# Smaller pieces for the preparation of lambda's powers, B's coefficients and the gate's scan in the first projection

## The chip, the cores and the metric

The kernel runs on one core of a Trainium2 chip. The metric is the device time of one execution in microseconds (us). The core has one in-order queue for each engine: PE (TensorE, the matmuls), DVE (VectorE), ACT (ScalarE), POOL (GpSimd) and SP (SyncE, which issues most DMAs). An engine starts the next instruction of its queue when that one's inputs are there; whatever stands behind a waiting instruction waits too.

## The reference, cut to what matters

Two layers over a sequence of 256 frames with a model width of 2048: first a gated linear attention (GLA), then a diagonal state-space layer (S5). Each layer modulates its input by a conditioning vector (adaLN), widens it to 4096, and ends in a residual LayerNorm.

```python
mod = einsum('bd,lde->lbe', silu(c), ada_w) + ada_b
for i in range(2):
    shift, scale, gate = split(mod[i], 3)
    u = x * (1 + scale) + shift
    h = gla_mixer(u, ...) if i == 0 else s5_mixer(u, ...)
    x = layer_norm(alpha * x + (1 + gate) * h, ln_g[i], ln_b[i])

# gla_mixer: the first projection, and the gate
q, k, v, z, g_lr = split(u @ w_in, ...)          # w_in: 2048 x 10256
log_alpha = log_sigmoid(g_lr @ gate_w2 + gate_b) / 16
# per chunk of 64 frames: cum = cumsum(log_alpha), k_dec = k * exp(tot - cum), ...

# s5_mixer: what can be prepared from the weights alone
dt = exp(log_dt)
mag = exp(a_re * dt)
lb_re, lb_im = mag * cos(a_im * dt), mag * sin(a_im * dt)      # lambda
coef = ((lb - 1) * conj(a)) / |a|^2                             # coef_re, coef_im
bb = coef * (b_re + 1j * b_im)                                  # B's coefficients
```

Everything is in float32 and has to be that exact, so each product is made from parts of reduced width (below).

## The kernel before, in words

The weights of every projection come in tiles of 128 x 1024 (two blocks of 128 input channels, k-blocks, by 512 output columns, 512 KB) through a ring of four buffers. Each tile is split into a high part `hi`, a copy made by ACT (L145), and a low part `lo = w - hi`, a subtraction on DVE (L146). PE then makes three products from them: `uh*hi`, `uh*lo`, `ul*hi`, where `uh` and `ul` are the same two parts of the modulated input. `hi` and `lo` have three buffers each. A tile of v is 12 matmuls of 512 columns (`mv_step`, L167 hi, L168 lo, L169 `ul`), a tile of q, k or z 24 matmuls of 256 columns (`st_step`, L180, L181, L182, of which L182 reads `lo`).

The first projection takes 96 tiles, called 0 to 95 here, in four blocks of u's 16 k-blocks (2, 2, 4 and 8 k-blocks), since u becomes available in this order. The third block is tiles 24 to 47: v in 24 to 39, q and k in 40 to 47. The fourth is tiles 48 to 95: q and k in 48 to 63, v in 64 to 95. At the end of each column group PE's sums are added to SBUF by DVE: `vbig` (L403) for v, `qk` (L417) for q and k. After tile 95 the attention scores (`psst`) and the z tiles follow.

Around the tiles the kernel hands over other work in pieces, in the Python loop that issues the tiles:

```python
            with tc.issue_after(last_lo[0]), tc.issue_after(last_mm[0]):
                for g_ in along.get(j, ()):
```

- `along`: the adaLN product (`psa`, `modsum`, `mods`) and the transposes of u (`psx`, `uf`, `u0l`), at fixed tiles.
- `lam`, a generator (`prep_lambda`): one piece after each tile of the third block. It works out lambda, its powers 1 to 8 (`pwr`, by the helper `tt`, L513, with scratch `pwt`), the coefficients (`crci`) and the packed eighth power (`psl`). `expx` is its exponential.
- `bg`, a list of pieces popped at a rate (`pump(V_RATE)`, in the fourth block): B's coefficients (`prep_b`, tiles `bb` and `bt`), their transposes (`psrb`), those of C, lambda's powers in rows (`prep_pow`, `pd`, `pspw`, `lc`), and weight sums of the later adaLN.
- `gate`, a generator (`gla_gate`): one piece a tile from the twentieth tile of the fourth block. Its scans along time are L739.

A piece ends at a `yield` (or at the end of a list's function). What is inside one piece is issued in one go; a scheduler then orders each engine's queue by when the inputs are expected to be ready, with the order of issue as its rule between ready ones. So the pieces decide which DVE instructions stand ahead of the `lo` of which tile.

Of the kernel before, what the change touches and what calls it, by code (L numbers as in the profile page):

```python
# [11 lines left out]
ALU = mybir.AluOpType  # L12
# [21 lines left out]
def trunk(ctx, tc, x, c, ln_g, ln_b, ada_w, ada_b, gla_w_in, gla_gate_w2, gla_gate_b, gla_norm_g,  # L34
# [3 lines left out]
    V, S, PE = nc.vector, nc.scalar, nc.tensor  # L38
# [35 lines left out]
    def s8t(name, shape, dt=F32):  # L74
        return s8.tile([P] + shape, dt, tag="s8", name=name)
# [382 lines left out]
    got = []  # L458
# [25 lines left out]

    SM = {}

    def expx(o, a, t1, t2, ti):

        V.tensor_scalar(a, a, 88.0, -87.0, op0=ALU.min, op1=ALU.max)
        V.tensor_scalar(t1, a, 1.4426950408889634, MAGIC, op0=ALU.mult, op1=ALU.add)  # L490
        V.tensor_scalar(t1, t1, MAGIC, None, op0=ALU.subtract)
        V.scalar_tensor_tensor(t2, t1, -0.693359375, a, op0=ALU.mult, op1=ALU.add)
        V.scalar_tensor_tensor(t2, t1, 2.12194440e-4, t2, op0=ALU.mult, op1=ALU.add)
        V.tensor_scalar(ti, t1, 127.0, 8388608.0, op0=ALU.add, op1=ALU.mult)
        V.tensor_scalar(o, t2, 1.9875691500e-4, 1.3981999507e-3, op0=ALU.mult, op1=ALU.add)
        for cf in (8.3334519073e-3, 4.1665795894e-2, 1.6666665459e-1, 5.0000001201e-1, 1.0, 1.0):
            V.tensor_tensor(o, o, t2, op=ALU.mult)
            V.tensor_scalar(o, o, cf, None, op0=ALU.add)
            if cf == 5.0000001201e-1:
                yield  # L500
        V.tensor_tensor(o, o, ti.bitcast(F32), op=ALU.mult)

    def prep_lambda():
        st = s8t("lamst", [16, 128])
        pw = s8t("pwr", [8, 2, 128])
        n_ = [0]

        def new():
            n_[0] += 1
            return st[:, n_[0] - 1, :]  # L510

        def tt(o, a, b, op):
            V.tensor_tensor(o, a, b, op=op)  # L513

        ar, ai = new(), new()
        dma(ar.rearrange("g (t p) -> g t p", t=2), s5_a_re[0].rearrange("(t g) p -> g t p", g=P))
        dma(ai.rearrange("g (t p) -> g t p", t=2), s5_a_im[0].rearrange("(t g) p -> g t p", g=P))
        dtt = tp.tile([P, 2], F32, tag="dtt", name="dtt", bufs=1)
        ld = tp.tile([2, P], F32, tag="ld", name="ld", bufs=1)
        dma(ld, s5_log_dt[0].rearrange("(t g) -> t g", g=P))  # L520
        for _ in range(3):
            yield
        ps = psx("psld")
        PE.transpose(ps[:, 0:2], ld, ident[:2, :2])
        sm = tp.tile([P, 4, 2], F32, tag="sm", name="sm", bufs=1)
        smi = tp.tile([P, 130], mybir.dt.int32, tag="smi", name="smi", bufs=1)
        S.copy(sm[:, 0], ps[:, 0:2])
        yield from expx(dtt, sm[:, 0], sm[:, 1], sm[:, 2], smi[:, 128:130])
        yield
        ag, mg, th = new(), new(), new()  # L530
        for t in range(2):
            V.tensor_scalar(ag[:, t * 64:t * 64 + 64], ar[:, t * 64:t * 64 + 64], dtt[:, t:t + 1], None, op0=ALU.mult)
            V.tensor_scalar(th[:, t * 64:t * 64 + 64], ai[:, t * 64:t * 64 + 64], dtt[:, t:t + 1], None, op0=ALU.mult)
        nn, r = new(), new()
        yield from expx(mg, ag, nn, r, smi[:, 0:128])
        yield
        V.tensor_scalar(nn, th, 1.0 / TWO_PI, MAGIC, op0=ALU.mult, op1=ALU.add)
        V.tensor_scalar(nn, nn, MAGIC, None, op0=ALU.subtract)
        V.scalar_tensor_tensor(r, nn, -C1, th, op0=ALU.mult, op1=ALU.add)
        V.scalar_tensor_tensor(r, nn, -C2, r, op0=ALU.mult, op1=ALU.add)  # L540
        V.scalar_tensor_tensor(r, nn, -C3, r, op0=ALU.mult, op1=ALU.add)
        V.tensor_scalar(r, r, 3.1415925, -3.1415925, op0=ALU.min, op1=ALU.max)
        sn, sh = new(), new()
        S.activation(sn, r, AF.Sin)
        S.activation(sh, r, AF.Sin, scale=0.5)
        yield
        cosm = new()
        tt(cosm, sh, sh, ALU.mult)
        V.tensor_scalar(cosm, cosm, -2.0, 1.0, op0=ALU.mult, op1=ALU.add)
        lr, li = pw[:, 0, 0, :], pw[:, 0, 1, :]  # L550
        tt(lr, mg, cosm, ALU.mult)
        tt(li, mg, sn, ALU.mult)
        nr, den, t1, t2 = new(), new(), new(), new()
        crci = tp.tile([P, 2, 128], F32, tag="crci", name="crci", bufs=1)
        cr, ci = crci[:, 0], crci[:, 1]
        V.tensor_scalar(nr, lr, -1.0, None, op0=ALU.add)
        tt(den, ar, ar, ALU.mult)
        tt(t1, ai, ai, ALU.mult)
        tt(den, den, t1, ALU.add)
        V.reciprocal(den, den)  # L560
        yield
        tt(t1, nr, ar, ALU.mult)
        tt(t2, li, ai, ALU.mult)
        tt(cr, t1, t2, ALU.add)
        tt(cr, cr, den, ALU.mult)
        tt(t1, li, ar, ALU.mult)
        tt(t2, nr, ai, ALU.mult)
        tt(ci, t1, t2, ALU.subtract)
        tt(ci, ci, den, ALU.mult)

        tm = s8t("pwt", [2, 4, 128])
        for m in (1, 2, 4):
            a_r, a_i = pw[:, 0:m, 0, :], pw[:, 0:m, 1, :]
            b_r = pw[:, m - 1:m, 0, :].to_broadcast([P, m, 128])
            b_i = pw[:, m - 1:m, 1, :].to_broadcast([P, m, 128])
            o_r, o_i = pw[:, m:2 * m, 0, :], pw[:, m:2 * m, 1, :]
            x1, x2 = tm[:, 0, 0:m, :], tm[:, 1, 0:m, :]
            tt(x1, a_r, b_r, ALU.mult)
            tt(x2, a_i, b_i, ALU.mult)
            tt(o_r, x1, x2, ALU.subtract)  # L580
            tt(x1, a_r, b_i, ALU.mult)
            tt(x2, a_i, b_r, ALU.mult)
            tt(o_i, x1, x2, ALU.add)
            yield
        SM.update(pw=pw, cr=cr, ci=ci)

        ps = psx("psl8")
        idv = ident.rearrange("g (f q b) -> g f q b", q=4, b=2)
        pv = ps[:, 0:256].rearrange("p (r h t n) -> p r h t n", r=2, h=2, t=2)
        for ri in range(2):  # L590
            for h in range(2):
                for t in range(2):
                    for q in range(4):
                        PE.matmul(pv[32 * q:32 * q + 32, ri, h, t, :],
                                  lhsT=pw[:, 7, ri, t * 64 + h * 32:t * 64 + h * 32 + 32], rhs=idv[:, :, q, :],
                                  start=True, stop=True)
        pr = ps[:, 0:256].rearrange("p (r k t n) -> p r t k n", r=2, k=2, t=2)
        for j, r, s in ((0, 0, 1.0), (0, 1, 1.0), (1, 0, 1.0), (1, 1, -1.0)):
            S.mul(l8[:, :, j, r].rearrange("p t (k n) -> p t k n", k=2), pr[:, j], s)
# [35 lines left out]
    def prep_b(t):  # L635
        got = {}

        def load():
            bi = s8t(f"bin{t}", [2, 64, 16])
            got["bi"] = bi  # L640
            dma(bi[:, 0], s5_b_re[0, t * P:(t + 1) * P])
            dma(bi[:, 1], s5_b_im[0, t * P:(t + 1) * P])

        def comp():
            bi = got["bi"]
            bb = s8t(f"bb{t}", [2, 64, 16])
            tm = s8t(f"bt{t}", [64, 16])
            cr = SM["cr"][:, t * 64:t * 64 + 64].unsqueeze(2).to_broadcast([P, 64, 16])
            ci = SM["ci"][:, t * 64:t * 64 + 64].unsqueeze(2).to_broadcast([P, 64, 16])
            V.tensor_tensor(bb[:, 0], bi[:, 0], cr, op=ALU.mult)  # L650
            V.tensor_tensor(tm, bi[:, 1], ci, op=ALU.mult)
            V.tensor_tensor(bb[:, 0], bb[:, 0], tm, op=ALU.subtract)
            V.tensor_tensor(bb[:, 1], bi[:, 1], cr, op=ALU.mult)
            V.tensor_tensor(tm, bi[:, 0], ci, op=ALU.mult)
            V.tensor_tensor(bb[:, 1], bb[:, 1], tm, op=ALU.add)
            got["b"] = bb.rearrange("g r p i -> g (r p) i")

        return [load], [comp] + to_rows(lambda: got["b"], lambda s, i: s[:, :, i], t, 256, f"b{t}")

    def prep_c(t):  # L660
        got = {}
# [23 lines left out]
    for part in range(2):  # L685
        for j in range(4):
            bg.extend(ada_dve(1, part, j))
    V_RATE, Z_RATE, OP_RATE = 0.62, 0.944, 0.755
    KEEP = (4, 6)
    GATE_AT = 20  # L690
    SCAN_RATE = 1.728
# [4 lines left out]
    def gla_gate():  # L696
# [20 lines left out]
        for f2 in range(4):  # L717
            ps = psx(f"psla{f2}")
            for i in range(2):
                f = 2 * f2 + i  # L720
                PE.matmul(ps[:, i * T:(i + 1) * T], lhsT=w2[:, f * P:(f + 1) * P], rhs=glr, start=True, stop=True)
            for i in range(2):
                f = 2 * f2 + i
# [13 lines left out]
        V.memset(rmask.rearrange("p (c t) -> p c t", c=4)[:, :, 0:1], 0.0)  # L737
        for f in range(8):
            V.tensor_tensor_scan(ea[:, f, :], rmask, la[:, f, :], 0.0, op0=ALU.mult, op1=ALU.add)  # L739
            if f == 3:  # L740
                yield
        yield
        cum = ea.rearrange("p f (c t) -> p (f c) t", c=4)
# [89 lines left out]
    for c0, w_, o in ((0, 4, 0), (1, 3, 4), (2, 2, 7)):  # L833
        a = s8t(f"qs{c0}", [8, w_, 64])
# [78 lines left out]
    for g in range(8):  # L913
# [9 lines left out]
        for f in range(4):  # L923
            i = (g * 4 + f) % 8
# [531 lines left out]
```

## Time and profile before

| what | value |
|---|---|
| time, median of 3 runs | 1836.67 us (1836.52 to 1839.31) |
| profiled execution | 1838.83 us, span 1837.1 us, mean granted clock 0.991 |
| PE busy | 1781.8 us (97%) |
| DVE busy | 1410.3 us (77%) |
| ACT busy | 895.4 us (49%) |
| POOL busy | 88.0 us (5%) |
| DMA | mean 249 GB/s, 457.86 MB |

The span is the time from the first to the last instruction, and the time of the execution is a little longer. Busy times are sums over instructions; a row of a timeline gives the start, the duration, the engine, the source line, the operation with what it writes and reads, and in brackets the idle time of the engine before it with what ended it. Rows of the timeline that stand next to each other overlap somewhat, because the engines are pipelined: the step from one start to the next says what an instruction costs in a row of them.

### The profile page before, as it was taken

How to read it: one execution, taken by the hardware profiler on the slowest of the kernel's cores; microseconds unless marked ns; L12 is line 12 of the kernel's file. 1: busy time of each engine (PE TensorE's matmuls, PEld its weight loads, DVE VectorE, ACT ScalarE, POOL GpSimd, SP SyncE). 2: the span in 40 equal slices, each digit the busy share in tenths (PEclk: the TensorE clock that was granted, in tenths of full speed). 3: DMA queues.
4: the chain of work that ended last, by engine and by line, in shares of the span. 5: the costliest groups of instructions: out<-in, count | busy, mean ns of one | idle time of the engine just before them, and what ended most of it. 6: DMA issues, size and time to landing. Idle time of an engine off the chain costs nothing.

```text
span 1837.1 us, 33664 instructions
## 1 busy us (share of the span) xinstructions
PE 1781.8 (97%) x13491; PEld 1574.5 (86%) x13491; DVE 1410.3 (77%) x1880; ACT 895.4 (49%) x1266; POOL 88.0 (5%) x94
## 2 busy tenths in 40 slices
PE   7999999999999999999999999999999999999997
PEld 5776897899999888899998999988888888888886
DVE  4887757879999988687699689888577775557556
ACT  4433557556556333654554535545445444444332
POOL 0000000000000000002233300000000000000000
PEclk9999999999999999999999999999999999999998
DMA  9997975879889998486665577999688886668653
GB/s 343 387 342 247 294 247 162 284 258 325 290 289 321 335 356 289 160 264 204 194 202 168 170 213 217 234 246 233 218 278 269 275 271 208 187 192 324 194 185 92
DMA packets 246101, 457.86 MB, mean 249 GB/s; under 512 B 19828, under 2 KB 49198, under 8 KB 244662
## 3 DMA queue, kind: packets, MB, share of 16 engines
q1 hardware_dynamic: 239320, 436.02, 74.1%
q0 software_dynamic: 5856, 18.63, 3.1%
q8 instruction: 106, 1.74, 0.4%
q10 hardware_dynamic: 768, 1.05, 0.2%
q14 instruction: 51, 0.42, 0.1%
HBM read 437.01 MB, written 18.61 MB: 248 GB/s over the span
## 4 chain that ended last, share of the span: by engine, by line
PE 78%; DVE 11%; DMA 4%; issue 3%; ACT 2%; POOL 0%; SPq 0%; DVEq 0%; ACTq 0%; POOLq 0%
PE gl L192 13%; PE gl L193 7%; PE op L168 6%; PE op L169 6%; PE op L167 6%; PE z L182 3%; PE z L181 3%; PE z L180 3%; PE v L168 3%; PE v L169 2%; PE v L167 2%; PE su L180 2%; PE su L181 2%; PE su L182 2%; PE sz L180 2%
## 5 line engine op out<-in xcount | busy, mean ns | idle before, releaser
L146 DVE TENSOR_TENSOR logl<-wgl,higl 128x1024 fp32r<-128x1024 f32 x128 | 156.7, 1224 | 116.0 <-ACT higl L145 111.2
L145 ACT CAST higl<-wgl 128x1024 fp32r<-128x1024 f32 x128 | 134.4, 1051 | 172.4 <-PE gl L192 167.5
L192 PE MATMUL gl<-yp,higl 128*128 128x512 f32 x512 | 179.4, 395 | 0.1
L192 PE MATMUL gl<-yb,higl 128*128 128x512 f32 x512 | 179.1, 395 | 0.0
L145 ACT CAST hio<-wo 128x1024 fp32r<-128x1024 f32 x95 | 100.2, 1055 | 152.8 <-PE op L169 131.9
L146 DVE TENSOR_TENSOR loo<-wo,hio 128x1024 fp32r<-128x1024 f32 x95 | 116.5, 1228 | 66.8 <-ACT hio L145 64.8
L317 DVE SCALAR_TENSOR_TENSOR acc<-wa,cs,acc 128x512 f32<-128x512 f32 x217 | 162.7, 750 | 2.9 <-DMA wa<-in_ada_w 0.2
L180 PE MATMUL sz<-u1h,hisz 128*128 128x256 f32 x512 | 150.4, 294 | 2.3 <-ACT zs L1284 2.3
L180 PE MATMUL su<-u1h,hisu 128*128 128x256 f32 x512 | 151.3, 297 | 0.0
L180 PE MATMUL z<-u0h,hiz 128*128 128x256 f32 x512 | 148.7, 290 | 0.0
L182 PE MATMUL sz<-u1h,losz 128*128 128x256 f32 x512 | 144.5, 283 | 2.1 <-DVE losz L146 2.1
L182 PE MATMUL su<-u1h,losu 128*128 128x256 f32 x512 | 145.8, 285 | 0.0
L181 PE MATMUL su<-u1l,hisu 128*128 128x256 f32 x512 | 145.6, 284 | 0.0
L182 PE MATMUL z<-u0h,loz 128*128 128x256 f32 x512 | 144.9, 283 | 0.6 <-DVE loz L146 0.6
L181 PE MATMUL z<-u0l,hiz 128*128 128x256 f32 x512 | 144.7, 283 | 0.0
L181 PE MATMUL sz<-u1l,hisz 128*128 128x256 f32 x512 | 144.7, 283 | 0.0
L193 PE MATMUL gl<-yb,logl 128*128 128x256 f32 x512 | 143.0, 279 | 0.0
L193 PE MATMUL gl<-yp,logl 128*128 128x256 f32 x512 | 142.3, 279 | 0.0
L145 ACT CAST hisz<-wsz 128x1024 fp32r<-128x1024 f32 x64 | 67.0, 1049 | 113.6 <-PE sz L181 57.4
L192 PEld LDWEIGHTS gl<-yp,higl 128*128 128x128 f32 x512 | 95.9, 188 | 22.9 <-issue 0.6
L192 PEld LDWEIGHTS gl<-yb,higl 128*128 128x128 f32 x512 | 96.0, 188 | 22.6
L145 ACT CAST hiz<-wz 128x1024 fp32r<-128x1024 f32 x64 | 67.2, 1051 | 88.2 <-PE z L181 80.8
(322 smaller groups left out, 5000.8 us busy)
## 6 DMA issues: line engine op xcount, KB each, us to landing
wgl<-in_s_w_glu SPq DMA_DIRECT2D x128, 512.0 KB, 4.8
wa<-in_ada_w SPq DMA_DIRECT2D x116, 512.0 KB, 5.2
wv<-in_gla_w_in SPq DMA_DIRECT2D x64, 512.0 KB, 6.5
wz<-in_gla_w_in SPq DMA_DIRECT2D x64, 512.0 KB, 5.4
wsu<-in_s_w_in SPq DMA_DIRECT2D x64, 512.0 KB, 4.5
wsz<-in_s_w_in SPq DMA_DIRECT2D x64, 512.0 KB, 5.7
wo<-in_s_w_out SPq DMA_DIRECT2D x64, 512.0 KB, 4.7
a<-in_ada_w SPq DMA_DIRECT2D x31, 1024.0 KB, 10.7
```

What stands on the lines that cost most here:

```text
L145: S.copy(hi, w)
L146: last_lo[0] = V.tensor_tensor(lo, w, hi.bitcast(F32), op=ALU.subtract).ins
L167: PE.matmul(banks[tt], lhsT=uh, rhs=hi[:, kk, :], start=(k == first), stop=False)
L168: PE.matmul(banks[tt], lhsT=uh, rhs=lo[:, kk, :], start=False, stop=False)
L169: last_mm[0] = PE.matmul(banks[tt], lhsT=ul, rhs=hi[:, kk, :], start=False, stop=(k == last)).ins
L180: PE.matmul(o, lhsT=wh, rhs=u.hi(k), start=(k == first), stop=False)
L181: PE.matmul(o, lhsT=wh, rhs=u.lo(k), start=False, stop=False)
L182: last_mm[0] = PE.matmul(o, lhsT=wl, rhs=u.hi(k), start=False, stop=(k == last)).ins
L192: PE.matmul(banks[f], lhsT=hi[:, kk, fs], rhs=u.both(k), start=(k == 0), stop=False)
L193: PE.matmul(banks[f][:, :T], lhsT=lo[:, kk, fs], rhs=u.hi(k), start=False, stop=(k == last))
L317: V.scalar_tensor_tensor(acc[0], w[:, kk, :], cs[:, k:k + 1], acc[0], op0=ALU.mult, op1=ALU.add)
```

## The change

The same arithmetic is handed over in more pieces. `prep_lambda` has 21 instead of 12, `prep_b`'s computation three instead of one, the gate's scans four of two instead of two of four. The rate of `bg` goes up from 0.62 to 0.704, so that the four added entries are popped within the same 48 tiles.

```diff
-    def expx(o, a, t1, t2, ti):
+    def expx(o, a, t1, t2, ti, stops=(5.0000001201e-1,)):
...
         V.scalar_tensor_tensor(t2, t1, 2.12194440e-4, t2, op0=ALU.mult, op1=ALU.add)
+        if len(stops) > 1:
+            yield
...
-            if cf == 5.0000001201e-1:
+            if cf in stops:
                 yield
...
-        yield from expx(mg, ag, nn, r, smi[:, 0:128])
+        yield
+        yield from expx(mg, ag, nn, r, smi[:, 0:128], (8.3334519073e-3, 1.6666665459e-1))
...
         V.tensor_scalar(nr, lr, -1.0, None, op0=ALU.add)
+        yield
         tt(den, ar, ar, ALU.mult)
...
         tt(cr, cr, den, ALU.mult)
+        yield
         tt(t1, li, ar, ALU.mult)
...
         tt(ci, ci, den, ALU.mult)
+        yield
 
         tm = s8t("pwt", [2, 4, 128])
         for m in (1, 2, 4):
...
             tt(x2, a_i, b_i, ALU.mult)
+            if m == 4:
+                yield
             tt(o_r, x1, x2, ALU.subtract)
+            if m == 2:
+                yield
             tt(x1, a_r, b_i, ALU.mult)
+            if m == 4:
+                yield
             tt(x2, a_i, b_r, ALU.mult)
...
-        def comp():
+        def comp(i):
...
+            if i == 0:
+                V.tensor_tensor(bb[:, 0], bi[:, 0], cr, op=ALU.mult)
+                V.tensor_tensor(tm, bi[:, 1], ci, op=ALU.mult)
+            elif i == 1:
+                V.tensor_tensor(bb[:, 0], bb[:, 0], tm, op=ALU.subtract)
+                V.tensor_tensor(bb[:, 1], bi[:, 1], cr, op=ALU.mult)
+            else:
+                V.tensor_tensor(tm, bi[:, 0], ci, op=ALU.mult)
+                V.tensor_tensor(bb[:, 1], bb[:, 1], tm, op=ALU.add)
...
-        return [load], [comp] + to_rows(...)
+        return [load], [lambda i=i: comp(i) for i in range(3)] + to_rows(...)
...
-    V_RATE, Z_RATE, OP_RATE = 0.62, 0.944, 0.755
+    V_RATE, Z_RATE, OP_RATE = 0.704, 0.944, 0.755
...
             V.tensor_tensor_scan(ea[:, f, :], rmask, la[:, f, :], 0.0, op0=ALU.mult, op1=ALU.add)
-            if f == 3:
+            if f % 2 and f < 7:
                 yield
```

The queues of ACT, SP and PE differ in where a few instructions stand, that of POOL not at all; what changes most is DVE's. In the rows below a name carries a running number, and the low part of a tile is `lov_` or `loq_`.

DVE's queue before, around the low parts of tile 37 (`lov_1521`) and tile 38 (`lov_1545`), from the last part of lambda's coefficients on:

```order
L513 TENSOR_TENSOR pwt<-pwr 128x128
L513 TENSOR_TENSOR crci<-crci,lamst 128x128
L513 TENSOR_TENSOR pwt<-pwr 128x128
L146 TENSOR_TENSOR lov_1521<-wv_1320,hiv_1520 128x1024
L513 TENSOR_TENSOR pwr<-pwt 128x128
L513 TENSOR_TENSOR pwt<-pwr 128x256 x2
L513 TENSOR_TENSOR pwr<-pwt 128x2x128
L403 TENSOR_TENSOR vbig<-vbig,v_1463 128x512
L513 TENSOR_TENSOR pwt<-pwr 128x256 x2
L403 TENSOR_TENSOR vbig<-vbig,v_1464 128x512
L513 TENSOR_TENSOR pwr<-pwt 128x2x128
L146 TENSOR_TENSOR lov_1545<-wv_1352,hiv_1544 128x1024
```

DVE's queue now, around the low parts of tile 37 (`lov_1457`), tile 38 (`lov_1485`) and tile 39 (`lov_1518`):

```order
L146 TENSOR_TENSOR lov_1457<-wv_1301,hiv_1456 128x1024
L403 TENSOR_TENSOR vbig<-vbig,v_1432 128x512
L403 TENSOR_TENSOR vbig<-vbig,v_1433 128x512
L146 TENSOR_TENSOR lov_1485<-wv_1327,hiv_1484 128x1024
L146 TENSOR_TENSOR lov_1518<-wv_1372,hiv_1517 128x1024
L515 TENSOR_TENSOR pwr<-lamst 128x128 x2
L559 TENSOR_SCALAR lamst<-pwr 128x128
L515 TENSOR_TENSOR lamst<-pwr,lamst 128x128
```

Lambda's burst moved from ahead of tile 37's low part to behind tile 39's; tile 38's low part still follows the two `vbig` sums of the column group that tile 37 ends.

DVE's queue before, where the low parts of tile 43 (`loq_1731`) and tile 44 (`loq_1782`) stand; `q_1683` to `q_1686` are the sums that tile 43 ends:

```order
L146 TENSOR_TENSOR loq_1731<-wq_1540,hiq_1730 128x1024
L238 TENSOR_REDUCE modsum_1676<-psmod_1671 128x4
L241 TENSOR_TENSOR mods<-modsum_1676,abT 128x4
L372 TENSOR_SCALAR uf_1720<-psx_1715,mods 128x256
L372 TENSOR_SCALAR uf_1724<-psx_1715,mods 128x256
L417 SCALAR_TENSOR_TENSOR qk_114<-q_1683,qk_114 128x256
L146 TENSOR_TENSOR loq_1782<-wq_1571,hiq_1781 128x1024
```

DVE's queue now from tile 43's low part (`loq_1690`) to tile 44's (`loq_1743`); `q_1640` to `q_1643` are the sums that tile 43 ends:

```order
L146 TENSOR_TENSOR loq_1690<-wq_1480,hiq_1689 128x1024
L515 TENSOR_TENSOR pwt<-pwr 128x256 x2
L372 TENSOR_SCALAR uf_1677<-psx_1672,mods 128x256
L515 TENSOR_TENSOR pwr<-pwt 128x2x128
L372 TENSOR_SCALAR uf_1681<-psx_1672,mods 128x256
L515 TENSOR_TENSOR pwt<-pwr 128x512 x2
L417 SCALAR_TENSOR_TENSOR qk_114<-q_1640,qk_114 128x256
L417 SCALAR_TENSOR_TENSOR qk_114<-q_1641,qk_114 128x256
L417 SCALAR_TENSOR_TENSOR qk_114<-q_1642,qk_114 128x256
L417 SCALAR_TENSOR_TENSOR qk_114<-q_1643,qk_114 128x256
L515 TENSOR_TENSOR pwr<-pwt 128x4x128
L146 TENSOR_TENSOR loq_1743<-wq_1515,hiq_1742 128x1024
```

Before, one `qk` sum and two `uf` stood between the two low parts; now four `qk` sums, two `uf` and six instructions of lambda's powers do.

PE's queue now at the start of tile 44, whose high part is `hiq_1742`:

```order
L365 MATMUL psx_1721<-ident,xrow_154 128x128
L180 MATMUL q_1738<-u0h_109,hiq_1742 128x256
L181 MATMUL q_1738<-u0l_111,hiq_1742 128x256
L180 MATMUL q_1739<-u0h_109,hiq_1742 128x256
L181 MATMUL q_1739<-u0l_111,hiq_1742 128x256
L180 MATMUL q_1740<-u0h_109,hiq_1742 128x256
L181 MATMUL q_1740<-u0l_111,hiq_1742 128x256
L180 MATMUL q_1741<-u0h_109,hiq_1742 128x256
L181 MATMUL q_1741<-u0l_111,hiq_1742 128x256
L182 MATMUL q_1738<-u0h_109,loq_1743 128x256
```

Eight matmuls that need only the high part now come first in this tile; before, the third one read the low part.

DVE's queue before, around the gate's scans and the low parts of tiles 79 (`lov_3012`) and 80 (`lov_3038`):

```order
L739 SCALAR_TENSOR_TENSOR ea<-rmask,la 128x256 x4
L146 TENSOR_TENSOR lov_3012<-wv_3009,hiv_3011 128x1024
L739 SCALAR_TENSOR_TENSOR ea<-rmask,la 128x256 x4
L146 TENSOR_TENSOR lov_3038<-wv_3035,hiv_3037 128x1024
L403 TENSOR_TENSOR vbig<-vbig,v_2929 128x512
```

DVE's queue now, around the low parts of tiles 79 (`lov_2997`), 80 (`lov_3028`) and 81 (`lov_3054`):

```order
L756 SCALAR_TENSOR_TENSOR ea<-rmask,la 128x256 x2
L146 TENSOR_TENSOR lov_2997<-wv_2994,hiv_2996 128x1024
L756 SCALAR_TENSOR_TENSOR ea<-rmask,la 128x256 x2
L146 TENSOR_TENSOR lov_3028<-wv_3025,hiv_3027 128x1024
L756 SCALAR_TENSOR_TENSOR ea<-rmask,la 128x256
L403 TENSOR_TENSOR vbig<-vbig,v_2925 128x512
L756 SCALAR_TENSOR_TENSOR ea<-rmask,la 128x256
L146 TENSOR_TENSOR lov_3054<-wv_3051,hiv_3053 128x1024
```

Two scans instead of four stand ahead of each of these low parts, and the last four scans come one or two tiles later.

More of the change, by code (lines that the diff above doesn't have):

```diff
@@ L642, in load @@
             dma(bi[:, 1], s5_b_im[0, t * P:(t + 1) * P])
-        def comp():
+        def comp(i):
             bi = got["bi"]
-            bb = s8t(f"bb{t}", [2, 64, 16])
-            tm = s8t(f"bt{t}", [64, 16])
+            if i == 0:
+                got["bb"] = s8t(f"bb{t}", [2, 64, 16])
+                got["tm"] = s8t(f"bt{t}", [64, 16])
+                got["b"] = got["bb"].rearrange("g r p i -> g (r p) i")
+            bb, tm = got["bb"], got["tm"]
             cr = SM["cr"][:, t * 64:t * 64 + 64].unsqueeze(2).to_broadcast([P, 64, 16])
             ci = SM["ci"][:, t * 64:t * 64 + 64].unsqueeze(2).to_broadcast([P, 64, 16])
[L650 to L658, printed above, removed]
+            if i == 0:
+                V.tensor_tensor(bb[:, 0], bi[:, 0], cr, op=ALU.mult)
[6 more added lines that the diff above has]
+                V.tensor_tensor(bb[:, 1], bb[:, 1], tm, op=ALU.add)
+        return [load], [lambda i=i: comp(i) for i in range(3)] + to_rows(lambda: got["b"], lambda s, i: s[:, :, i], t, 256, f"b{t}")
     def prep_c(t):
```

## The prediction

> **What bounds the kernel now.** I read the page's busy shares first, then the waits of PE by stage, then the timelines of PE and DVE where those waits lie.
>
> ```profile
> PE 1781.8 (97%) x13491; PEld 1574.5 (86%) x13491; DVE 1410.3 (77%) x1880; ACT 895.4 (49%) x1266; POOL 88.0 (5%) x94
> ```
>
> PE is busy for 97% of the span, so the change, which alters no matmul, can win only where PE stops. The waits of PE from 130 to 200 us, and then from 270 to 340 us:
>
> ```profile
> PE v L168 <- DVE lov L146: 3.8, 2, 1.9
> ...
> PE v L168 <- DVE lov L146: 1.7, 3, 0.7
> PE psrb L627 <- DVE bb L655: 0.5, 1, 0.5
> ```
>
> 6.0 us in all, each time for DVE. The timelines say what stood ahead of the low parts. PE at tiles 37 and 38, then DVE there:
>
> ```profile
> 151.34 0.39 PE L169 MATMUL v<-hiv,u0l 128*128 128x512 f32 x1
> 151.57 0.61 PE L167 MATMUL v<-hiv,u0h 128*128 128x512 f32 x2
> 154.09 0.50 PE L168 MATMUL v<-lov,u0h 128*128 128x512 f32 x1 [1.91 <-DVE lov L146]
> 154.43 0.40 PE L169 MATMUL v<-hiv,u0l 128*128 128x512 f32 x1
> ...
> 156.53 0.62 PE L167 MATMUL v<-hiv,u0h 128*128 128x512 f32 x2
> 159.06 0.50 PE L168 MATMUL v<-lov,u0h 128*128 128x512 f32 x1 [1.91 <-DVE lov L146]
> ...
> 160.44 0.63 PE L169 MATMUL v<-hiv,u0l 128*128 128x512 f32 x1
> 160.87 0.63 PE L168 MATMUL v<-lov,u0h 128*128 128x512 f32 x1
> ...
> 163.00 0.44 PE L167 MATMUL v<-hiv,u0h 128*128 128x512 f32 x1
> ```
>
> ```profile
> 149.65 0.49 DVE L513 TENSOR_TENSOR pwr<-lamst 128x128 f32<-128x128 f32 x2
> ...
> 152.81 1.23 DVE L146 TENSOR_TENSOR lov<-wv,hiv 128x1024 fp32r<-128x1024 f32 x1
> ...
> 156.18 0.76 DVE L513 TENSOR_TENSOR pwt<-pwr 128x256 f32<-128x256 f32 x2
> 156.85 0.68 DVE L403 TENSOR_TENSOR vbig<-vbig,v 128x512 f32<-128x512 f32 x1
> 157.45 0.42 DVE L513 TENSOR_TENSOR pwr<-pwt 128x256 f32<-128x256 f32 x1
> 157.78 1.22 DVE L146 TENSOR_TENSOR lov<-wv,hiv 128x1024 fp32r<-128x1024 f32 x1
> 158.92 1.29 DVE L513 TENSOR_TENSOR pwt<-pwr 128x512 f32<-128x512 f32 x2
> 160.12 1.22 DVE L146 TENSOR_TENSOR lov<-wv,hiv 128x1024 fp32r<-128x1024 f32 x1
> 161.25 0.69 DVE L513 TENSOR_TENSOR pwr<-pwt 128x512 f32<-128x512 f32 x1
> ```
>
> The matmuls step by 0.23 us, so a v tile takes 12 x 0.2275 = 2.73 us. Tile 37 took 156.53 - 151.57 = 4.96, a loss of 2.23: lambda's burst held DVE from 149.65 to 152.81. Tile 38 took 6.47, a loss of 3.74: a second wait of 2.23, and 1.5 of half clock, seen in the rows of 0.63 us that step by 0.43. From the start of a low part to PE's resumption it is 1.28 us both times (152.81 to 154.09, 157.78 to 159.06).
>
> **Lambda's pieces, tiles 37 and 38.** No instruction is added; 3.16 us of DVE work and what follows it move behind the low part of tile 39. Tile 37's low part now takes the burst's place at 149.65 and reaches PE by 150.9, which wants it at 152.0 (151.57 and two steps): gain 2.23. Tile 38's low part still stands behind both vbig sums, and the second of those waits for PE to end tile 37: in the rows it starts 0.32 after tile 38's start (156.85 against 156.53) and holds DVE for 0.60. So PE resumes 0.32 + 0.60 + 1.28 = 2.20 after the tile's start, where it wants to go on after two matmuls, 0.46. With 0.11 for the slower first matmul (0.34 to the next start instead of 0.23) the loss is 1.85: gain 0.38. Both together gain 2.61.
>
> **Where lambda's powers go: tiles 43 to 46.** The powers now lie among the q tiles. The nearest prices of their rows, and of what they stand beside, and PE's rows of tile 44:
>
> ```profile
> 183.40 1.08 DVE L417 SCALAR_TENSOR_TENSOR qk<-q,qk 128x256 f32<-128x256 f32 x3
> 184.40 1.22 DVE L146 TENSOR_TENSOR loq<-wq,hiq 128x1024 fp32r<-128x1024 f32 x1
> 188.96 0.99 DVE L372 TENSOR_SCALAR uf<-psx,mods 128x256 f32<-128x256 f32 x2
> ...
> 183.57 0.28 PE L182 MATMUL q<-u0h,loq 128*128 128x256 f32 x1
> 183.69 0.60 PE L365 MATMUL psx<-ident,xrow 128*128 128x128 f32 x4
> 184.05 0.36 PE L180 MATMUL q<-u0h,hiq 128*128 128x256 f32 x1
> ```
>
> From the end of tile 43's low part to the start of tile 44's DVE does, by steps: pwt 0.67, two uf 1.0, pwr 0.33, pwt 1.20, four qk 1.33, pwr 0.69, together 5.2; PE resumes 1.28 later, at 6.5. Meanwhile PE has tile 43 with its transposes (24 matmuls of 0.12 and 0.36: 3.3) and eight matmuls of tile 44 (0.95): 4.3. So PE stops by up to 2.2. From below: the last qk needs the last sum of tile 43, so it cannot end before about 184.40 in before's terms; then pwr 0.7 and 1.28 give 186.4, against 184.05 + 0.95 = 185.0: at least 1.4. I take 2.0, since nothing ahead of this chain gives DVE room, and 0.1 more for tile 43. Tiles 45 and later have room: in this table by stages (PE, PE's loads, DVE, ACT, POOL, clock, DMA) DVE was busy for 17.05 of 25 us from 175 to 200, and PE never stopped.
>
> ```profile
> 175.00:200.00 25.00, 25.00 (x208) 20.13 (x207) 17.05 (x31) 9.13 (x13) 0.00 (x0) 1.00 0.92 326
> ...
> 315.00:360.00 45.00, 45.00 (x212) 37.28 (x211) 39.12 (x47) 23.74 (x24) 2.30 (x2) 1.00 0.79 253
> ```
>
> The a tiles that SP issues there no longer wait for lambda's scratch, and load earlier: at nothing, as PE waits for none. `psl` and `prep_pow` come up to 20 us later; their readers wait for nothing else of it before the fourth block: nothing.
>
> **The clock.** Of two equal gaps, the one at 154.09 was followed by full speed (0.40), that at 159.06 by half; a gap of 2.10 later in the run was also followed by half, in these rows of PE (the same work took 0.62 before it):
>
> ```profile
> 1208.51 0.62 PE L1259 MATMUL psy<-wc,xS 128*32 128x128 f32 x16
> ...
> 1214.51 0.66 PE L1256 MATMUL psy<-mt,U 128*32 128x128 f32 x8 [2.10 <-DMA mt<-dk]
> 1214.90 1.11 PE L1259 MATMUL psy<-wc,xS 128*32 128x128 f32 x16
> ```
>
> So a gap near 1.9 costs about 1.6 or nothing, by its place in a window that the kernel does not set; I take one half each. Before had two such gaps (on average 1.6); after has one near 1.9 at tile 44 (0.8) and one of about 1.5 at tile 38 (nothing, as gaps of 0.4 to 0.7 in the next fence also cost none). Gain 0.8 on average, with ends of -1.6 (it falls on after only) and +1.6. As the profiled execution had this dip and stood 2.16 above the median, the median may hold less of it: I take 0.5.
>
> The Trainium skill ("TensorE: Matmul & The Clock Gate", in "Part 1: The HAM clock gate") has the array fall to half rate after at least one idle window of about 3.4 us, free-running, and puts it in "HAM oscillation" as no PE-idle gaps above 3.4 us. By this a gap of 1.9 costs nothing and the sum would lack the 0.5; the row at 159.06 speaks against it.
>
> **The gate's scans, tiles 79 and 80.** PE and DVE there:
>
> ```profile
> 310.81 0.50 PE L168 MATMUL v<-lov,u0h 128*128 128x512 f32 x1 [0.63 <-DVE lov L146]
> ...
> 314.27 0.50 PE L168 MATMUL v<-lov,u0h 128*128 128x512 f32 x1 [0.67 <-DVE lov L146]
> ```
>
> ```profile
> 307.20 2.44 DVE L739 TENSOR_TENSOR_SCAN ea<-rmask,la 128x256 f32<-128x256 f32 x4
> 309.55 1.20 DVE L146 TENSOR_TENSOR lov<-wv,hiv 128x1024 fp32r<-128x1024 f32 x1
> ...
> 313.01 1.21 DVE L146 TENSOR_TENSOR lov<-wv,hiv 128x1024 fp32r<-128x1024 f32 x1
> ```
>
> Four scans step by 2.35, two by 1.17. Tile 79's low part then starts at 308.4 instead of 309.55, tile 80's at 310.7 instead of 313.0; the waits to cover are 0.63 + 0.11 and, on top of that, 0.67 + 0.11. Both vanish: gain 1.5. The other four scans fall among tiles 81 and 82, at most 1.2 of DVE work added to each, at the edge of the stage from 315 to 360 us (row above) where PE was never idle and DVE had 5.9 us free. The wait at tile 77 (1.7 - 0.63 - 0.67, about 0.4) and that of psrb (0.5) stay, since the queue up to there is unchanged.
>
> **B's pieces.** The same six DVE instructions in the same order, so nothing at tile 77; nothing too at tile 56, where a low part already stood between them.
>
> **Given back at the end.** PE reaches the end of tile 95 earlier, but the first z tiles are bound by a transfer:
>
> ```profile
> 360.40 1.99 ACT L145 CAST hiz<-wz 128x1024 fp32r<-128x1024 f32 x2 [3.93 <-DMA wz<-in_gla_w_in]
> 362.35 0.47 ACT L851 COPY sts<-psst 64x384 f32<-64x384 f32 x1
> ```
>
> The copies of the scores stand behind it. Its load is issued when earlier tiles release their buffers, so it moves too, if not wholly: between 0 and the 1.9 gained in stalls; I take 0.3.
>
> **Sum.** 2.61 - 2.1 + 0.5 + 1.5 - 0.3 = 2.2. From the median 1836.67: 1834.4. Against the profiled execution it is 1838.83 - 1.7 = 1837.1 with a dip at tile 44, and 1.6 less without, 1835.5; those runs and the three shown differ by as much as the whole sum. About 0.2% (3.7 us) is what a measurement can tell from no change, so this counts as none.
>
> **Rivals.**
> - More is gained (0.30): tile 44's stop is at its lower end, 1.4, the z load moves along, and the clock stays full: 2.61 - 1.5 + 1.6 + 1.5 = 4.2, 1832.5. For it: DVE's room behind tile 45 shows that it is not late on average. Against: each part must fall well.
> - Slower (0.10): lambda's powers are not covered among the q tiles at all. Moved behind tile 39 are the burst, 3.16, and the powers after it, by the steps above two times 0.67 + 0.33 + 1.20 + 0.69: 5.8, together 9.0. If every one delays a low part there, PE loses 9.0 where it lost 4.5 before: 1836.67 + 4.5 + 1.6 (a dip) - 1.5 = 1841.3. It decides against the change from 4.5 + 1.5 = 6.0 of stops between tiles 40 and 48 on. Against it: 8 us of DVE idle in the row from 175 to 200.
> - Nothing arrives (0.12): the scans' 1.5 is swallowed by the wait for wz, and the clock gives nothing: 2.61 - 2.1 = 0.5, 1836.2.
> - The page's rule on the clock (0.03): only stops count, 2.61 - 2.1 + 1.5 - 0.3 = 1.7, 1835.0.
>
> **How the numbers follow.** The forecast, 1834.4, has 0.45. Its own range is 1832 to 1837; with the other cases I give 1829.5 to 1839.5, which leaves out the worst of the slower case and a gain beyond the sum of all stops (6.0) and a dip. Faster is the first rival and a little of the forecast's lower end: 0.32. Slower by over 0.2% is 0.09; the same 0.59.
>
> **What would show it.** No wait at tile 37; 1.5 to 1.6 at tile 38; a new one of 1.3 to 2 on `loq` at tile 44, released by DVE; none on `lov` at tiles 79 and 80; 0.4 and 0.5 still at tile 77 and psrb; half clock at one place or none near 180 us. Wrong if tile 44 does not stop, if a q tile beside it does for longer than 2.2, or if the time at which the z tiles start has not moved by as much as the stops.

## The result and the profile after

| | before | after |
|---|---|---|
| median, 6 runs each | 1837.35 us (1835.43 to 1839.43) | 1832.15 us (1830.59 to 1833.42) |
| profiled execution | 1838.83 us, span 1837.1 | 1832.45 us, span 1830.7 |

The ratio is 0.997, its 95% interval 0.9958 to 0.9983: the change makes the kernel faster, by 5.2 us between the medians and by 3.1 to 7.7 us by the interval. The forecast of 1834.4 was 2.2 too slow; its range holds the time, but the likeliest case, "no change that a measurement can tell", did not come.

The page's line of busy shares after, and PE's waits from 130 to 200, from 200 to 270 and from 270 to 340 us:

```profile
PE 1781.4 (97%) x13491; PEld 1575.3 (86%) x13491; DVE 1410.2 (77%) x1880; ACT 896.2 (49%) x1266; POOL 88.1 (5%) x94
```

```profile
PE q L182 <- DVE loq L146: 1.6, 1, 1.6
PE v L168 <- DVE lov L146: 1.5, 1, 1.5
...
PE pspw L625 <- ACT lc L627: 2.9, 2, 2.2
...
PE psrb L639 <- DVE bb L673: 0.5, 1, 0.5
PE v L168 <- DVE lov L146: 0.4, 1, 0.4
```

The work is the same to a microsecond. Four of the five stops that DVE's low parts caused before are gone or smaller, one new one stands on `loq`, and one, at `pspw`, has grown. PE at tiles 36 to 38 and at tile 44, in the timeline after:

```profile
152.43 0.62 PE L167 MATMUL v<-hiv,u0h 128*128 128x512 f32 x2
152.89 0.39 PE L168 MATMUL v<-lov,u0h 128*128 128x512 f32 x1
...
155.15 0.61 PE L167 MATMUL v<-hiv,u0h 128*128 128x512 f32 x2
157.23 0.50 PE L168 MATMUL v<-lov,u0h 128*128 128x512 f32 x1 [1.46 <-DVE lov L146]
157.57 0.40 PE L169 MATMUL v<-hiv,u0l 128*128 128x512 f32 x1
...
182.12 0.38 PE L182 MATMUL q<-u0h,loq 128*128 128x256 f32 x1 [1.56 <-DVE loq L146]
```

Tile 37 runs without a stop in 155.15 - 152.43 = 2.72 us; tile 38 stops for 1.46; tile 44 for 1.56. Behind both gaps PE goes on at full speed (0.40, 0.38): the half clock of the profile before does not come.

To place the gain, the later comparisons use three marks that every kernel here has: the last `psmod` before tile 36, the eight `psx` at tile 48, and the first `psst` behind tile 95. The view of a tile gives the first and last start behind the durations. Before, then after:

```profile
L236 PE MATMUL psmod<-ident,row x4: 271/272/273, 144.1 to 144.4; 128*128 128x128 f32 x4
L365 PE MATMUL psx<-ident,xrow x8: 270/272/273, 200.5 to 201.2; 128*128 128x128 f32 x8
L849 PE MATMUL psst<-qs,qk x48: 272/326/430, 360.7 to 365.9; 128*64 128x256 f32 x16, 128*64 128x192 f32 x16, 128*64 128x128 f32 x16
```

```profile
L236 PE MATMUL psmod<-ident,row x4: 271/272/273, 144.7 to 145.0; 128*128 128x128 f32 x4
L365 PE MATMUL psx<-ident,xrow x8: 270/272/273, 198.2 to 199.0; 128*128 128x128 f32 x8
L866 PE MATMUL psst<-qs,qk x48: 272/326/430, 357.3 to 362.7; 128*64 128x256 f32 x16, 128*64 128x192 f32 x16, 128*64 128x128 f32 x16
```

The first stretch, with lambda in it, took 56.4 us before and 53.5 after; the second, with B and the scans, 160.2 and 159.1. That is 4.0 us. The other 2.4 us of the two spans' 6.4 are the net of differences elsewhere; the largest of them lies between 1200 and 1300 us, in the second layer, where the change moves nothing (PE is idle there for 5.2 us before and 2.6 after, rows below).

### The profile page after: what moved, and what is told of

The parts are those of the page before. It is cut to its first block, busy times and chain, and to the rows that moved or that the text cites. A ratio compares the mean times of both kernels' runs of the same rounds, so it can differ in the third digit from the quotient of the medians.

```text
span 1830.7 us, 33667 instructions
## 1 busy us (share of the span) xinstructions
PE 1781.4 (97%) x13491; PEld 1575.3 (86%) x13491; DVE 1410.2 (77%) x1880; ACT 896.2 (49%) x1266; POOL 88.1 (5%) x94
## 4 chain that ended last, share of the span: by engine, by line
PE 77%; DVE 11%; DMA 6%; issue 3%; ACT 2%; SPq 0%; POOL 0%; DVEq 0%; ACTq 0%; POOLq 0%
PE gl L192 13%; PE gl L193 7%; PE op L168 6%; PE op L169 6%; PE op L167 6%; PE v L168 3%; PE v L169 3%; PE v L167 3%; PE z L182 3%; PE z L181 3%; PE z L180 3%; PE su L180 2%; PE su L181 2%; PE su L182 2%; PE sz L180 2%
## 5 line engine op out<-in xcount | busy, mean ns | idle before, releaser
L317 DVE SCALAR_TENSOR_TENSOR acc<-wa,cs,acc 128x512 f32<-128x512 f32 x215 | 160.5, 746 | 5.7 <-DMA wa<-in_ada_w 2.9
```

The costliest lines, as they stand in the source:

```text
L317: V.scalar_tensor_tensor(acc[0], w[:, kk, :], cs[:, k:k + 1], acc[0], op0=ALU.mult, op1=ALU.add)
```

## The experiments

Three theories went in. A: the gain is what the stops of PE in the first projection cost. B: most of it comes from the second layer's stage after 1200 us, which any shift sets off. C: it is the clock's half windows alone. All kernels by the two stretches, each from the same three rows of its own profile. The ratio of after is against the six executions of before in the table above, those of e1 to e4 against 29 others, that of e10 against 11 others; a kernel that was run once has its single time instead:

| kernel | first stretch | second stretch | time against before, 95% interval |
|---|---|---|---|
| before | 56.4 | 160.2 | |
| before again | 57.8 | 160.3 | one run, 1835.34 us |
| after | 53.5 | 159.1 | 0.997 (0.9958 to 0.9983) |
| after again | 53.5 | 159.0 | one run, 1835.26 us |
| e1, lambda's pieces only | 53.5 | 160.3 | 0.9978 (0.9966 to 0.9991) |
| e2, the scans only | 56.4 | 158.4 | 0.9992 (0.9982 to 1.0003) |
| e3, B's pieces only | 55.5 | 159.3 | 0.9991 (0.998 to 1.0003) |
| e4, after, sums behind the low part | 50.9 | 158.3 | 0.9948 (0.9932 to 0.9964) |
| e7, after, powers unsplit | 55.6 | 157.8 | one run, 1831.89 us |
| e8, before, sums behind the low part | 57.0 | 160.5 | one run, 1834.76 us |
| e9, after, wg early | 53.5 | 157.4 | one run, 1833.48 us |
| e10, e4 and wg early | 50.9 | 157.4 | 0.9948 (0.9933 to 0.9964) |

**The parts alone.** In each of the three kernels the two other parts of the diff are undone.

```diff
 e1: -            if f % 2 and f < 7:          e2: lambda's stops and
     +            if f == 3:                       B's pieces undone
     B in one piece, V_RATE 0.62               e3: lambda's stops and the scans undone
```

> Lambda's 21 pieces alone; B's computation in one piece, its rate 0.62, the scans in two pieces of four. Theory A (the gain is the stops of PE in the first projection, each worth what the rows say): no wait at tile 37 (2.1 less), 1.4 to 1.5 at tile 38, 1.6 at tile 44 (1.7 more), the small matmuls psl 0.7 shorter, half clock after tile 38 gone where it was; waits at tiles 79 and 80 (0.6, 0.7) as before. Up to 290 us of the trace 1.5 to 2.0 earlier than before apart from the clock; in the median 1.5 to 3 us faster. Theory B (the larger part of the gain comes from the second layer's stage after 1200 us, where after waited 2.6 us for mt and before 5.1, and any shift of the first projection brings it): at least 3 us more between 1200 and 1290 us of the trace, 4 to 6 us faster. Theory C (all is the clock's half windows): no difference where no half window differs.

> The gate's scans in four pieces alone. A: waits at tiles 37 and 38 as before (1.9, 1.9), none at tiles 79 and 80: the trace 1.5 to 1.9 earlier from 320 us on, 0.2 of it given back at the first z tiles; median 1.3 to 1.9 faster. B: 3 us more between 1200 and 1290 us, 4 to 5 faster. C: no difference but for half windows.

> B's computation in three pieces and the rate 0.704 alone. A: all waits of the first projection as before, the matmuls pspw up to 0.7 later or not at all; median within 0.8 us of before. B: as the queue of DVE hardly changes, 0 to 3 us by the second layer's stage. C: 0.

e1 has after's first stretch to 0.1 us and before's second. e2 has before's first stretch (with its two waits of 1.9 and the half clock) and a second one 1.8 shorter; its waits at tiles 79 and 80 are gone, with PE's rows from 300 to 316 us showing only these two:

```profile
302.06 0.50 PE L168 MATMUL v<-lov,u0h 128*128 128x512 f32 x1 [0.44 <-DVE lov L146]
305.56 1.14 PE L627 MATMUL psrb<-ident,bb 128*128 128x128 f32 x8 [0.44 <-DVE bb L661]
```

e3's second stretch is 0.9 shorter than before's, which A had expected to be up to 0.7 longer: `pspw` waits less. PE's waits from 200 to 270 us in before, then in e3:

```profile
PE pspw L613 <- ACT pd L606: 1.0, 1, 1.0
PE pspw L613 <- ACT lc L615: 0.8, 2, 0.4
```

```profile
PE pspw L613 <- ACT lc L615: 1.2, 2, 0.6
```

Its first stretch is 0.9 shorter by the clock, below. The intervals of e2 and e3 take in no change, so only their stretches, not their times, tell them from before. So lambda's pieces bring 2.9 in the first stretch, and in the second the scans bring 1.8 and B's pieces 0.9. These last two do not add up in the changed kernel, which gains 1.1 there and not 2.7; what they collide with is shown below with the gate's weights. e1's time gained 4.0 us (1.6 to 6.2). Its 2.9 fits that, but so do B's 4 to 6, and in its profile PE is idle for only 0.3 us from 1200 to 1300; e1 alone does not decide between A and B.

**The same kernels again.**

> The kernel before, unchanged, for a second profile of it. A: the same waits in the first projection (1.9 and 1.9 at tiles 37 and 38, 0.6 and 0.7 at 79 and 80), a half window at most once near 155 to 163 us; from 1200 to 1290 us of the trace 2 to 6 us less than in the first profile of before, as in every kernel since, because what the first profile lost there was a draw. B: the second layer's stage loses the same 4 us again, and only the changed kernels are quick there.

> The changed kernel, unchanged, for a second profile. A: the stretch from 146 to 200 us as in its first profile to 0.1 us, that from 290 to 358 too (1.85 less than before); no half window from 140 to 220 us, since no gap there reaches 1.9. B and C: the stretches differ between the two profiles by a us or more.

From 1200 to 1300 us, in the table by stages (PE's busy time is the first number behind the stretch's length), in this order before, before again, after, after again:

```profile
1200.00:1300.00 100.00, 94.83 (x1266) 87.70 (x1265) 85.59 (x101) 57.24 (x91) 0.00 (x0) 0.98 0.94 243
```

```profile
1200.00:1300.00 100.00, 97.87 (x1294) 90.44 (x1294) 86.58 (x104) 59.92 (x93) 0.00 (x0) 1.00 0.95 252
```

```profile
1200.00:1300.00 100.00, 97.41 (x1283) 89.54 (x1282) 84.96 (x100) 58.66 (x91) 0.00 (x0) 1.00 0.95 251
```

```profile
1200.00:1300.00 100.00, 93.17 (x1217) 85.93 (x1218) 82.73 (x99) 57.20 (x89) 0.00 (x0) 1.00 0.94 240
```

PE is idle for 5.2 and 2.1 us in the one kernel, for 2.6 and 6.8 in the other, most of it at `psy`, which waits there for the transfer of `mt` or what follows on it. It is a draw of the execution, whatever the kernel: theory B falls. It can hide the whole gain of one execution: the one of after again took 1835.26 us, no less than before again's 1835.34, though its two stretches together are 5.6 shorter. In the first projection both kernels repeat: after's stretches come out at 53.5 twice and at 159.1 and 159.0; before's second at 160.2 and 160.3. Only before's first stretch differs, by 1.4, and its rows say why. PE at tiles 37 and 38 in the second profile of before:

```profile
152.61 0.50 PE L168 MATMUL v<-lov,u0h 128*128 128x512 f32 x1 [1.91 <-DVE lov L146]
153.56 0.63 PE L168 MATMUL v<-lov,u0h 128*128 128x512 f32 x1
...
159.00 0.50 PE L168 MATMUL v<-lov,u0h 128*128 128x512 f32 x1 [1.78 <-DVE lov L146]
160.03 0.61 PE L169 MATMUL v<-hiv,u0l 128*128 128x512 f32 x1
```

Here both gaps are followed by half speed; in the first profile only the second was. The expectation of "a half window at most once" was wrong.

**The low part ahead of the sums.** e4 is the changed kernel with the group's sums held back until the next tile's low part has been issued; e8 does the same to the kernel before.

```diff
-                        V.tensor_tensor(o, o, banks[cg][tt], op=ALU.add)
+                        hold(lambda o=o, b=banks[cg][tt]: V.tensor_tensor(o, o, b, op=ALU.add))
...
+            got = split(w, wants[j][2])
+            with tc.issue_after(last_lo[0]):
+                while held:
+                    held.pop(0)()
```

(`qk`'s sums likewise.)

> The changed kernel, and the sums vbig and qk of a column group are issued behind the low part of the next tile, so that tile 38's low part stands ahead of the two vbig sums and tile 44's ahead of the four qk sums and the last pwr. A: the wait at tile 38 vanishes (1.6 less), that at tile 44 falls from 1.6 to 0.2 at most (1.4 to 1.7 less): another 3 us faster than the change, 6 to 9 faster than before. B: the same as the change or a random shift of 0 to 4 by the second layer's stage. C: as the change's, with no half window left near 160 and 180 us.

> The kernel before with the sums behind the next low part, and lambda in its large pieces. A: as the burst still stands ahead of tile 37's low part, the wait there stays 1.9; at tile 38 DVE has the two sums (1.2) moved behind and more products ahead of the low part, 1.0 to 1.9 of wait remain; the stretch from 146 to 200 us at most 1 us shorter than before, so the order of the sums alone does not bring e4's gain. B, C: a random shift.

e4 is the fastest kernel here together with e10: 0.9948, 9.5 us less than before (6.6 to 12.5), of which its two stretches show 7.4. DVE and then PE in its trace:

```profile
147.63 2.35 DVE L146 TENSOR_TENSOR lov<-wv,hiv 128x1024 fp32r<-128x1024 f32 x2
151.34 0.69 DVE L412 TENSOR_TENSOR vbig<-vbig,v 128x512 f32<-128x512 f32 x1 [1.35 <-PE v L169]
152.47 0.69 DVE L412 TENSOR_TENSOR vbig<-vbig,v 128x512 f32<-128x512 f32 x1 [0.45 <-PE v L169]
```

```profile
175.53 0.39 PE L182 MATMUL q<-u0h,loq 128*128 128x256 f32 x1 [0.42 <-DVE loq L146]
```

Tile 38's low part now ends before the two sums that wait for PE, and from 130 to 200 us PE has one wait left, 0.42 at tile 44, where at most 0.2 had been expected. The first stretch is 2.6 shorter than after's. In the kernel before the same order brings nothing (57.0 against 56.4 and 57.8), since lambda's burst stands ahead of the low parts there; the wait at tile 38 is even longer than was expected. PE's wait from 130 to 200 us in e8:

```profile
PE v L168 <- DVE lov L146: 4.1, 2, 2.2
```

In these two kernels the order brings something only where the pieces are small.

**More work ahead of tile 44.** e7 takes the five stops out of the loop over the powers.

```diff
-            if m == 4:
-                yield
-            if m == 2:
-                yield
```

> The changed kernel without the five stops inside the loop of lambda's powers, so that one more pair of products of 512 (1.2) and one more pwr (0.7) stand ahead of tile 44's low part, and psl comes into tile 44. A: the stops of PE in tile 44, by psl and the low part together, grow from 1.6 to 3.0 to 3.6 us and a half window follows; the stretch from 146 to 200 us is 2 to 5 us longer than the changed kernel's. B and C: as the changed kernel but for a half window.

The stretch is 2.1 longer than after's, which is in the range of theory A, but in part for another reason. PE's waits in tile 44 sum up to 1.7 (1.0 for `loq`, 0.5 for a `qk` sum, 0.2 for `psl`), not 3 to 3.6, and no half clock follows. PE between tiles 46 and 47 in e7:

```profile
191.99 1.04 PE L277 MATMUL psa<-a,cz 128*32 128x512 f32 x2
192.97 0.31 PE L440 MATMUL psv<-ident,vr 104*128 104x104 f32 x1
193.20 1.92 PE L277 MATMUL psa<-a,cz 128*32 128x512 f32 x14
195.05 0.39 PE L180 MATMUL q<-u0h,hiq 128*128 128x256 f32 x1
```

DVE took as much longer between the two low parts as was worked out: 6.85 us (173.98 to 180.83) instead of 5.03 in after (175.81 to 180.84). PE filled part of it with `psl`, which stood in tile 44 in this kernel, and the rest came in three gaps. From the `psx` ahead of tile 43 to the `psa` behind tile 44 PE took 10.41 us (173.79 to 184.20), and 8.61 in after (175.61 to 184.22), 1.8 more. If `psl` is counted there with the 0.7 that after has for it later in the stretch, the delay of the low part cost about 1.1. The other 1.0 of the 2.1 has nothing to do with DVE: in e7 one `psv` fell into a `psa`, and the two took 3.06 us (191.99 to 195.05), where a `psa` alone takes 1.86. The expectation counted the delay and left out what PE could do meanwhile. In the second stretch e7 is 1.3 shorter than after, where `pspw` waits 1.7 in all and not 2.9.

**The gate's weights.** Between 200 and 290 us after is 0.6 slower than before, which the forecast did not have. ACT in the trace of after shows a cast that waits for a load, with `lc` behind it:

```profile
217.72 0.41 ACT L353 CAST wgp<-wg 128x256 fp32r<-128x256 f32 x1 [1.88 <-DMA wg<-in_gla_w_in]
218.03 1.04 ACT L145 CAST hiq<-wq 128x1024 fp32r<-128x1024 f32 x1
218.97 2.09 ACT L627 ACTIVATE lc<-pspw 128x512 f32<-128x512 f32 x2
```

e9 issues that load 18 tiles earlier in the loop; e10 does it in e4.

```diff
+                if i == 2:
+                    load_wg()
```

> The changed kernel, and the load of the gate's weights wg issued at the fourth block's third tile instead of its twentieth; nothing else moves but wgp's two instructions. A: what the changed kernel loses between 200 and 290 us of the trace (0.6 more than before) is lc standing behind wgp on ACT, which waits 1.9 for wg; without that wait the fourth pspw waits under 0.7 instead of 2.2, and the stretch gets 1.5 to 1.9 shorter, 0.9 to 1.3 less than before's. Rival: lc is late for its own four passes on ACT, whatever wgp does: pspw waits 2 us as it did, and the stretch keeps its length.

> The kernel with the sums behind the low part, and wg loaded early as well. A: the stretch from 146 to 200 us 5.7 shorter than before, that from 200 to 290 1.0 to 1.3, that from 290 to 358 1.9: 8.8 us without the draw elsewhere; median 8 to 12 us faster than before. Rival: as the kernel without the early load, 7.6 by the same stretches.

In e9 PE's waits from 200 to 270 us are:

```profile
PE pspw L625 <- ACT lc L627: 1.3, 2, 0.7
```

The second stretch is 1.7 shorter than after's (157.4 against 159.1), within what A expected. It is 2.8 shorter than before's, close to the 1.8 of the scans and the 0.9 of B's pieces together. So the parts collide in this one cast: in the traces of before, e1, e3 and e2 it stands behind all of `lc` on ACT (at 224.70, 221.07, 221.36 and 223.91 us), and only with all parts together did it move ahead of the last four passes of `lc`, where its load had not landed. Which two parts are enough for that was not tried. In e7 it stands there too but waits only 0.60, which fits e7's shorter second stretch. In e10 the second stretch is 0.9 shorter than e4's, but the time shows no difference (both 0.9948).

## Why the prediction was half right

Term by term, in us gained, forecast and shown:

| term | forecast | shown |
|---|---|---|
| tiles 37 and 38, stops | 2.61 | 2.7: tile 37 takes 2.72 instead of 4.96; tile 38 waits 1.46 instead of 1.91 |
| tiles 43 and 44 | -2.1 | -1.9: one wait of 1.56; from its `psx` to the next `psa` tile 44 takes 5.29 instead of 3.40 |
| clock | 0.5 | about 1.5, as what is left |
| `psl` | 0 | 0.7 |
| `pspw` | 0 | -0.6 |
| scans | 1.5 | 1.8 |
| given back at z | -0.3 | 0 to -0.2 |
| sum | 2.2 | 4.1 |

- **The moves were right.** The wait at tile 37 went, that at tile 38 stayed for the reason given (the sums ahead of it wait for PE: e4 removes it), the new one at tile 44 cost 1.9, between the two bounds of 1.4 and 2.2 (rows below; 183.69 is the start of its `psx` before), those at tiles 79 and 80 went, and tile 77 and `psrb` kept theirs. PE around tile 44 after, and the `psa` behind it before:

```profile
178.93 0.60 PE L365 MATMUL psx<-ident,xrow 128*128 128x128 f32 x4
...
184.22 1.92 PE L277 MATMUL psa<-a,cz 128*32 128x512 f32 x16
```

```profile
187.09 1.92 PE L277 MATMUL psa<-a,cz 128*32 128x512 f32 x16
```

- **The clock was the term most mis-sized.** The step gave a gap at tile 44 "near 1.9" half a chance of a half window. It was 1.56, and there was none behind it or behind tile 38's 1.46 in any profile of after, e1 and e9. And the kernel before had at least one half window between 150 and 164 us in all five profiles with its order of lambda (before twice, e2, e3, e8). The mean first stretch of before, before again, e2 and e3 is 56.5; 53.5 + 2.7 - 1.9 + 0.7 = 55.0 accounts for the rest without the clock, which leaves 1.5, the price that the prediction read off tile 38's rows for one half window. Two steps made the term too small: 0.8 was set against it for tile 44, and it was lowered to 0.5 because the profiled execution stood above the median. What stood above it was the draw after 1200 us (5.2 us idle against 2.1 in before again). Theory C falls as well, since e1, e2 and e4 gain by stops.
- **`psl` was costed at nothing**, because its readers come late. But its 64 matmuls themselves moved. In before they lay among a `psa`, together from 163.82 to 167.07, 3.25 us; a `psa` alone takes 1.86 to the next start (159.76 to 161.62 in after). That leaves 1.4 for `psl`, where in after it takes 0.7 (194.51 to 195.20). PE in before, then in after:

```profile
163.82 0.46 PE L594 MATMUL psl<-ident,pwr 128*32 128x32 f32 x32
164.10 1.45 PE L277 MATMUL psa<-a,cz 128*32 128x512 f32 x9
...
166.08 1.06 PE L277 MATMUL psa<-a,cz 128*32 128x512 f32 x5
167.07 0.50 PE L167 MATMUL v<-hiv,u0h 128*128 128x512 f32 x1
```

```profile
159.76 1.92 PE L277 MATMUL psa<-a,cz 128*32 128x512 f32 x16
161.62 0.50 PE L167 MATMUL v<-hiv,u0h 128*128 128x512 f32 x1
...
194.51 0.76 PE L606 MATMUL psl<-ident,pwr 128*32 128x32 f32 x64
195.20 0.66 PE L236 MATMUL psmod<-ident,row 128*128 128x128 f32 x4
```

- **`pspw`: the cover that was named was the wrong one.** The readers of the powers wait for nothing of lambda, but ACT, in order, waited for `wg` ahead of `lc`, a place in ACT's queue that the forecast did not price. e9 shows it. The term is a net of two: B's pieces save 0.9 (e3), and the wait for `wg` costs about 1.6.
- **The scans were sized by the idle in brackets.** The step took 0.63 and 0.67 and 0.11 each for the restart. From start to start it is more. The matmuls of before ahead of the two gaps were:

```profile
309.79 0.39 PE L167 MATMUL v<-hiv,u0h 128*128 128x512 f32 x1
...
313.21 0.39 PE L169 MATMUL v<-hiv,u0l 128*128 128x512 f32 x1
```

  To 310.81 it is 1.02 instead of 0.23, to 314.27 1.06; with 0.11 each that makes 1.84, which is what e2 and after gained from `psrb` to the first `psst` (1.89 and 1.85). The bracket counts from the modelled end of a matmul, 0.39 after its start, while the next could start after 0.23.
- The first rival (1832.5, a gain of 4.2) came nearest the time, and in the main for the reasons it gave: the clock stayed full and the z tiles moved along. Only tile 44 was not at its lower end; that `psl` and `pspw`, which it did not have, nearly cancel (0.7 and -0.6) is luck. The slower rival fell: DVE's work among the q tiles was covered but for tile 44. "Nothing arrives" fell: the first z matmul moved from 366.76 to 363.54 us. The rival by the Trainium skill's rule on the clock ("TensorE: Matmul & The Clock Gate", "Part 1: The HAM clock gate": half rate after at least one idle window of about 3.4 us) fell by the half windows behind gaps of 1.9 us.

The sum by stages, 4.1, lies within the interval of the measured gain, 3.1 to 7.7. The rest to 5.2 is probably a draw of the six executions of before: the 29 and the 11 others have medians of 1835.52 and 1835.49 us, against which after's median is 3.4 lower. These were not taken beside after, so it is not shown; no stretch of the two pairs of profiles shows a further gain that repeats.

## What to carry to other kernels

An in-order engine that prepares the next tile should not have ahead of that preparation something that waits for the current tile; splitting a burst helps as far as the pieces fall in idle time, and the order against the waiting sums is worth as much again (2.6 us in e4). When work is moved, read each queue it is moved in for the instruction that waits there for a transfer, and cost a stop of a pipelined engine from start to start. A part of the difference between two profiles may be a draw; a second profile of each kernel can tell which, at the price of one execution. And run the parts of a change alone as well as together: together they can move an instruction that none of them moves alone, as the cast of `wg` here (1.6 us).

## What the runs showed of the hardware

The clock fell to half for one window (3.41 us in the trace's clock) behind gaps of 1.8 to 2.2 us between 150 and 160 us in five profiles of five with lambda's old order, and twice in one of them; behind the 1.46 and 1.56 of after it never did. Nor did it behind every longer one: in these five profiles tiles 37 and 38 have nine gaps of 1.78 to 2.16 us, of which six were followed by half speed. The place of the window sets the price: in e3 it came behind the first gap and made the second one shorter (1.40), so that the first stretch was 0.9 shorter than before's, while before again, with two of them, was 1.4 longer. The Trainium skill ("TensorE: Matmul & The Clock Gate", "Part 1: The HAM clock gate") has a whole idle window of about 3.4 us as the condition; these rows show half speed behind an idle time of little more than half of that.
